# Hybrid decoder step on one core: the last pair of column blocks as block products, the reciprocal root's chain on VectorE, the layer vectors loaded early and turned later

## The chip, the cores and the metric

The kernel runs on one core of a Trainium2 chip, as one program. The metric is the device time of an execution in microseconds (us). A core has TensorE (PE in the profile; PEld is its weight load), VectorE (DVE), ScalarE (ACT), GpSimd (POOL) and SyncE (SP), each with an instruction queue of its own that it works through in order; they meet at semaphores.

## What is computed

Two layers of a decoder, for a prompt of 512 tokens and 8 samples of 4 tokens (544 tokens in all), model width 1024, feed-forward width 2816. In float32:

```python
def layer_norm(x, g, b):
    mu = mean(x); var = mean(square(x - mu))
    return (x - mu) * rsqrt(var + LN_EPS) * g + b

def swiglu(x, w_up, w_down):
    a, u = split(x @ w_up, 2)
    return (silu(a) * u) @ w_down

def decoder_layer(x, ...):
    x = layer_norm(ALPHA * x + 0.5 * swiglu(x, ffn1_up, ffn1_down), ln1_g, ln1_b)
    q, k, v, glu, gates = split(x @ w_in + b_in)
    attn = window_attention(q, k, v, sinks)            # 128 tokens back, ALiBi
    c = silu(layer_norm(causal_depthwise(u_a * sigmoid(u_g)), conv_ln_g, conv_ln_b))
    mix = sigmoid(g_attn) * (attn @ w_attn_out) + sigmoid(g_conv) * (c @ w_conv_out)
    x = layer_norm(ALPHA * x + mix @ w_out, ln2_g, ln2_b)
    x = layer_norm(ALPHA * x + 0.5 * swiglu(x, ffn2_up, ffn2_down), ln3_g, ln3_b)
```

The outputs are the activations and the new caches (keys, values, convolution state) of both groups.

## The kernel before

The activations stand transposed: features on the 128 partitions, the 544 tokens in the free dimension, as four tiles of two feature blocks each. Token halves are 272 wide (`CUT`; in the last FFN's end 288 and 256). Every large product is done three times over split numbers: weights and activations are each split into a high part (a cast to fp32r by ScalarE) and a low part (what is left, by a subtraction on VectorE), and high x high, high x low and low x high are summed in PSUM.

A *plain unit* (`unit`, L451 to L453) is one piece of 256 weight columns times one token half: for each of `kk` blocks of 128 input features and each of two column blocks of 128, three matmuls. A piece is fetched by SP and split by `prep` (L291, L292). `W` takes prepared pieces in order and prepares `la` pieces ahead; `ahead(n)` does so at a fixed place.

*FFNs.* Of the four FFNs three are *fast* (`is_fast`: all but layer 0's first). All start with `up_first`: the column blocks 0 and 1 of `a` and `u` as plain units. Then, in a fast FFN, `middle` walks through `fast_order`. An entry `s(j, m)` is a *product run*: 128 columns of `a` and the same 128 of `u`. The weights are read as 2 x 2 block matrices (the two input blocks of a pair, by `a` and `u`), the activations likewise (the two input blocks, by the two token halves), and their product takes seven block products instead of eight. The activations' four combinations for it are the tiles `T`, made in the stage before by `right`; the weights' combinations are made by `steps`. `up_fast` issues a run: one matmul that opens a buffer (L678), then the seven products (L664; each 4 x 3 matmuls of 272 columns), with copies, sums and the SiLU between them (L682 to L696). The returned `rest` (L702, L460, L461) multiplies the gate and splits the result into `H`. An entry `dn` is a plain unit of the down projection, over one group of column pairs (`GROUPF`, the last group holds three pairs, `kk` = 6). Pairs 2 to 9 are done by product runs. Pair 10 follows as plain units: `a` 10 and `u` 10, both halves each (192 matmuls). Then `tail` does the last group's `dn` units, first half before second, with the layer norm.

*The planner.* In `middle` the preparation is cut into steps with a cost on ScalarE and VectorE (`steps`) and a number of buffers. `fill(us)`, called behind each product and unit, advances a time and emits steps as long as their summed costs keep up with it and `room` is left; `room` counts free buffers of the pool `pair` (37 buffers). `V` takes the next prepared piece and forces steps if it isn't ready. `more` keeps three pieces fetched, up to the piece `stop`. Instructions of `middle` are kept in program order; elsewhere (also in `tail`) a scheduler orders each engine's instructions by an estimate of its own, when the program is built. That order is fixed when it runs.

*Layer norm.* `ln_fin` gives three steps, emitted a set distance apart while the next units are issued (`put_off`, `due`; the distances are `D_LN`, in units in which one block of six matmuls counts 0.7) or at the stage's end (`flush`): `centre` sums over the partitions with a matmul (L482), subtracts the mean (L487) and squares; `newton` sums the squares (L500, matmuls L504) and calls `rsqrt`; `scale` spreads the root over the partitions with matmuls (L512), multiplies (L516) and hands on to `ln_out` (gain and bias L549, splits L460, L461). `rsqrt` works on at most 128 x 3 numbers: three instructions on VectorE (L526 to L528: add epsilon, and the seed from the number's bits), then eleven on POOL (L530 to L540), each of which but the first needs the one before. There are 16 roots: 14 from `ln_fin`, two in `final`, the output stage, which turns the last sums back (L878), takes statistics (L880, L886) and applies mean, gain, root and bias (L893, L902).

*Layer vectors.* `setup_layer` loads the layer's gains, biases, convolution weights and sinks by small DMAs on POOL's queue (L983 to L1015), turns them with TensorE (L992, L1001) into PSUM buffers of the pool `ps1` (two buffers) and copies them out with VectorE (L994, L1002); a third use of `ps1` holds a small matmul (L1012). Its source tiles come from the pool `f1` (ten buffers). `mark` calls it behind `up_first` in the first FFN of a layer; in layer 1 it also issues the cache shifts.

## Time and profile before

| | us |
|---|---|
| median of 3 runs | 2626.16 |
| lowest, highest | 2626.13, 2630.38 |
| the profiled execution | 2630.69 |
| its span, first to last instruction | 2628.7 |

The profile is of one execution. Its rows are times from the span's start. A row of the timeline gives start, duration, engine, line, operation, what it writes and reads, how many instructions are merged, and in brackets the idle time before it with what ended it. TensorE's matmuls overlap, so the distance between two starts, not the duration, is what one costs. [...]

### The profile page before, as it was taken

To read this page: it belongs to the slowest core of one execution; us is meant where nothing else is said; L and a number is where in the kernel's file an instruction comes from. 1 tells how busy PE (TensorE), PEld (TensorE's weight loads), DVE (VectorE), ACT (ScalarE), POOL (GpSimd) and SP (SyncE) were. 2 spreads that over 40 slices of the span, in tenths; PEclk is the share of its full clock that TensorE was granted. 3 is DMA by queue.
4 is the path that set the end of the run, shared out by engine and by line. 5 is a ranking of instruction groups with operands and counts; after the bars stand their busy time and mean duration, and the time that the engine had idled before them with its cause. 6 is when DMAs were issued, how large, how long until landed. Compare 5 with 4: busy or idle time off the path is not lost.

```text
span 2628.7 us, 47397 instructions
## 1 busy us (share of the span) xinstructions
PE 2552.5 (97%) x20110; PEld 2502.8 (95%) x20110; DVE 1715.0 (65%) x2567; ACT 1126.2 (43%) x1972; POOL 298.0 (11%) x499
## 2 busy tenths in 40 slices
PE   8999999999999999999989999989999999999996
PEld 7999999988999999999989999989899999999996
DVE  4333237797986567666556666549979766676645
ACT  4222124477526254443344443245773353444431
POOL 2000001722301000000020000017232000000001
PEclk8999999999999999999989999989999999999998
DMA  7223133231322213332422333312214222233331
GB/s 219 83 89 104 54 109 85 50 95 53 101 65 87 91 58 96 97 97 89 133 75 82 97 97 97 116 49 76 82 53 113 69 81 87 78 93 97 97 101 39
DMA packets 302628, 232.15 MB, mean 88 GB/s; under 512 B 43812, under 2 KB 300020, under 8 KB 302320
## 3 DMA queue, kind: packets, MB, share of 16 engines
q1 hardware_dynamic: 298576, 220.37, 27.8%
q0 software_dynamic: 3840, 8.76, 1.1%
q8 instruction: 157, 2.57, 0.4%
q14 instruction: 55, 0.45, 0.1%
HBM read 225.69 MB, written 9.16 MB: 89 GB/s over the span
## 4 chain that ended last, share of the span: by engine, by line
PE 82%; DVE 8%; POOL 4%; ACT 3%; issue 2%; DMA 1%; DVEq 0%; POOLq 0%; ACTq 0%
PE pa L453 20%; PE pa L451 20%; PE pa L452 20%; PE pa L664 11%; PE pb L664 8%; DVE pr L1126 3%; POOL f L1141 2%; DVE wl L292 1%; DVE pr L461 1%; PE pb L1266 1%; DVE at L1247 1%; PE pa L1237 1%; PE pb L1278 1%; ACT at L1251 1%; PE pb L512 0%
## 5 line engine op out<-in xcount | busy, mean ns | idle before, releaser
L451 PE MATMUL pa<-pr,wh 128*128 128x272 f32 (+1 forms) x4032 | 1176.1, 293 | 18.7 <-ACT pr L460 11.1
L453 PE MATMUL pa<-pr,wl 128*128 128x272 f32 (+1 forms) x4032 | 1173.4, 292 | 4.9 <-DVE wl L292 4.9
L452 PE MATMUL pa<-pr,wh 128*128 128x272 f32 (+1 forms) x4032 | 1170.3, 291 | 3.7 <-DVE pr L461 3.6
L451 PEld LDWEIGHTS pa<-pr,wh 128*128 128x128 f32 x4032 | 765.8, 190 | 26.0 <-ACT pr L460 13.5
L452 PEld LDWEIGHTS pa<-pr,wh 128*128 128x128 f32 x4032 | 771.5, 191 | 8.2 <-DVE pr L461 6.0
L453 PEld LDWEIGHTS pa<-pr,wl 128*128 128x128 f32 x4032 | 765.6, 190 | 6.1 <-DVE wl L292 5.7
L292 DVE TENSOR_TENSOR wl<-raw,wh 128x1024 fp32r<-128x1024 f32 (+1 forms) x268 | 309.8, 1183 | 77.3 <-ACT wh L291 54.0
L1126 DVE SCALAR_TENSOR_TENSOR pr<-u,cw,pr 128x512 f32<-128x512 f32 x480 | 344.4, 764 | 2.2 <-ACT pr L1119 2.0
L291 ACT CAST wh<-raw 128x1024 fp32r<-128x1024 f32 (+1 forms) x268 | 259.9, 1009 | 159.8 <-PE pa L453 90.9
L453 PE MATMUL pa<-pr,wd 128*128 128x272 f32 x768 | 221.8, 289 | 0.0
L451 PE MATMUL pa<-pr,wd 128*128 128x272 f32 x768 | 221.4, 288 | 0.0
L452 PE MATMUL pa<-pr,wd 128*128 128x272 f32 x768 | 220.8, 288 | 0.0
L717 DVE SCALAR_TENSOR_TENSOR pr<-pa,pr 128x544 f32<-128x544 f32 (+2 forms) x152 | 109.7, 722 | 153.5 <-PE pa L453 152.7
L530 POOL TENSOR_SCALAR nw<-nw 91x3 f32<-91x3 f32 (+2 forms) x16 | 5.6, 349 | 1703.2 <-DVE nw L526 1703.2
L460 ACT CAST pr<-f 128x544 fp32r<-128x544 f32 (+1 forms) x124 | 79.7, 647 | 216.4 <-DVE f L611 116.1
L664 PE MATMUL pa<-pr,wa 128*128 128x272 f32 x1152 | 160.9, 289 | 0.0
L664 PE MATMUL pb<-pr,ws 128*128 128x272 f32 x1152 | 159.6, 288 | 0.0
L664 PEld LDWEIGHTS pa<-pr,wa 128*128 128x128 f32 x1152 | 151.4, 188 | 0.0
L664 PEld LDWEIGHTS pb<-pr,ws 128*128 128x128 f32 x1152 | 150.0, 188 | 0.0
L452 PEld LDWEIGHTS pa<-pr,wd 128*128 128x128 f32 x768 | 145.1, 189 | 0.0
L451 PEld LDWEIGHTS pa<-pr,wd 128*128 128x128 f32 x768 | 144.5, 188 | 0.0
L453 PEld LDWEIGHTS pa<-pr,wd 128*128 128x128 f32 x768 | 144.3, 188 | 0.0
(225 smaller groups left out, 3139.6 us busy)
## 6 DMA issues: line engine op xcount, KB each, us to landing
raw<-in_ffn_up_dram SPq DMA_DIRECT2D x174, 512.0 KB, 4.4
raw<-in_ffn_down_dram SPq DMA_DIRECT2D x76, 512.0 KB, 3.6
raw<-in_w_in_dram SPq DMA_DIRECT2D x72, 512.0 KB, 4.1
raw<-in_w_in_dram SPq DMA_DIRECT2D x64, 128.0 KB, 3.0
raw<-in_w_attn_out_dram SPq DMA_DIRECT2D x32, 256.0 KB, 4.0
raw<-in_w_conv_out_dram SPq DMA_DIRECT2D x16, 512.0 KB, 3.4
raw<-in_w_out_dram SPq DMA_DIRECT2D x16, 512.0 KB, 4.3
raw<-in_ffn_down_dram SPq DMA_DIRECT2D x24, 256.0 KB, 2.8
```

The costliest lines, as they stand in the source:

```text
L291: ins = self.nc.scalar.copy(wh, t)
L292: self.nc.vector.tensor_tensor(wl, t, wh.bitcast(F32), op=ALU.subtract)
L451: pin(self.nc.tensor.matmul(o, lhsT=wh, rhs=h, start=k == 0, stop=False))
L452: pin(self.nc.tensor.matmul(o, lhsT=wh, rhs=lo, start=False, stop=False))
L453: pin(self.nc.tensor.matmul(o, lhsT=wl, rhs=h, start=False, stop=k == kk - 1))
L460: pin(self.nc.scalar.copy(hi, src))
L461: pin(self.nc.vector.tensor_tensor(lo, src, hi.bitcast(F32), op=ALU.subtract))
L664: mm = lambda a, b, first=False, last=False: pin(nc.tensor.matmul(o, lhsT=a, rhs=b, start=first, stop=last, skip_group_check=True))
L717: pin(nc.vector.scalar_tensor_tensor(Y[p][:, :, hs], ps, 0.5, Y[p][:, :, hs], op0=ALU.mult, op1=ALU.add))
L1126: self.last["cw"] = nc.vector.scalar_tensor_tensor(cc[:, m, 0:SEQ], u[:, m, k:k + SEQ], cw[:, 8 * k + c:8 * k + c + 1], cc[:, m, 0:SEQ], o ...
L1141: nc.gpsimd.tensor_tensor(pr[:, 4 * b:4 * b + 4, :], win, wv.unsqueeze(1).to_broadcast([128, DS, KC]), op=ALU.mult)
L1237: nc.tensor.matmul(s[:, 2 * r + t, :], lhsT=q, rhs=k, start=t == 0 and ps == 0, stop=ps == 2, skip_group_check=True)
```

## The change

- `fast_order` ends with the two product runs `s(10, 0)` and `s(10, 1)` in place of `a` 10 and `u` 10; `middle` walks through them too, the plain units of pair 10 and the method `P` are gone, and the planner's `stop` takes in the last group's four `dn` pieces, which `pre` now takes with `V` instead of preparing them with `ahead(4)`.
- `rsqrt` issues its eleven instructions on VectorE instead of POOL.
- `setup_layer` issues its DMAs and returns a function `turn` that does the transposes, copies and the small matmul. In a fast FFN (layer 1) the loads are issued ahead of `up_first` and `turn` and the cache shifts come behind it; in layer 0 both come where they came before. The two halves of the convolution weights share one tile, and the sinks' small tile has a tag of its own.

```diff
--- before.py
+++ after.py
@@ fast_order
-        return o + [("a", 10), ("u", 10)] + [("dn", 4, p, 0) for p in range(4)]
+        return o + [s(10, 0), s(10, 1)] + [("dn", 4, p, 0) for p in range(4)]
...
@@ rsqrt
         self.nc.vector.tensor_scalar(i32(r), i32(t), -1.0, float(RS_SEED), op0=ALU.mult, op1=ALU.add)
-        g = self.nc.gpsimd
+        g = self.nc.vector
         g.tensor_scalar_mul(u, v, RS_B * RS_B)
...
@@ ffn, begin
-            self.stop = self.pi + len(self.ffn_order(l, f)) - 10
+            self.stop = self.pi + len(self.ffn_order(l, f)) - 4
...
@@ ffn, middle
-            for kind, *k in self.fast_order()[4:-6]:
+            for kind, *k in self.fast_order()[4:-4]:
...
@@ ffn
         if self.is_fast(l, f):
             gl = len(GROUPF) - 1
+            turn = self.mark(l, f)
             up_first()
             Y += self.scaled(Y0)
-            self.mark(l, f)
+            turn()
             middle()
             if last:
                 self.cut = FB[FK[1][0]][0]
-            wa = self.P(l, f, "a", 10)
-            h = new_h(gl)
-            sa = [silu(wa, 0)]
-            self.ahead(2)
-            sa.append(silu(wa, 1))
-            wu = self.W(l, f, "u", 10, la=1)
-            gated(wu, h, 0, sa[0])
-            self.ahead(2)
-            gated(wu, h, 1, sa[1])
             ws = []
 
             def pre(hf):
                 if hf == 0:
-                    self.ahead(4)
-                    ws.extend(self.W(l, f, "dn", gl, p, la=1) for p in range(4))
+                    ws.extend(self.V(l, f, "dn", gl, p) for p in range(4))
                 else:
                     self.ahead(A3)
...
@@ ffn, the other branch
-                    self.mark(l, f)
+                    self.mark(l, f)()
...
@@ mark
-        if f == "ffn1":
-            if l == 0:
-                self.setup2()
-            self.setup_layer(l)
+
+        if f != "ffn1":
+            return lambda: None
+        if l == 0:
+            self.setup2()
+        turn = self.setup_layer(l)
+
+        def rest():
+            turn()
             if l:
                 self.shift_caches(l)
+        return rest
...
@@ setup_layer
-        ps = self.p1()
-        nc.tensor.transpose(ps[:, :NVEC], rows[:NVEC, :], self.ident[:NVEC, :NVEC])
-        vec = t([128, NVEC], F32, f"vec{l}")
-        nc.vector.tensor_copy(vec, ps[:, :NVEC])
-        cw = t([128, KC * 8], F32, "cw")
         wr = a["conv_dw_w"][l].rearrange("k (c p) -> (k c) p", p=128)
-        ps = self.p1()
+        wrows = self.f1(shape=[128, 2, 128])
         for h in range(2):
-            rows = self.f1(shape=[128, 128])
-            nc.gpsimd.dma_start(rows[:124, :], wr[124 * h:124 * h + 124, :])
-            nc.tensor.transpose(ps[:, 124 * h:124 * h + 124], rows[:124, :], self.ident[:124, :124])
-        self.after(nc.vector.tensor_copy(cw, ps[:, :248]), "cw")
+            nc.gpsimd.dma_start(wrows[:124, h, :], wr[124 * h:124 * h + 124, :])
...
-        sk4 = self.sp.tile([128, 4], F32, tag="nw", name=self.nm("nw"))
+        sk4 = self.sp.tile([128, 4], F32, tag="sk", name=self.nm("sk"))
...
+
+        def turn():
+            ps = self.p1()
+            nc.tensor.transpose(ps[:, :NVEC], rows[:NVEC, :], self.ident[:NVEC, :NVEC])
+            vec = t([128, NVEC], F32, f"vec{l}")
+            nc.vector.tensor_copy(vec, ps[:, :NVEC])
+            cw = t([128, KC * 8], F32, "cw")
+            ps = self.p1()
+            for h in range(2):
+                nc.tensor.transpose(ps[:, 124 * h:124 * h + 124], wrows[:124, h, :], self.ident[:124, :124])
+            self.after(nc.vector.tensor_copy(cw, ps[:, :248]), "cw")
+            nc.vector.tensor_scalar_mul(nsk, nsk, -1.0)
+            nsks = t([128, 4], F32, f"nsks{l}")
+            ps = self.p1()
+            nc.tensor.matmul(ps[:, :4], lhsT=sel, rhs=sk4[:4], start=True, stop=True)
+            nc.vector.tensor_copy(nsks, ps[:, :4])
...
+        return turn
```

## Rows read from the trace of the kernel before

**Rows 1.** The page, busy time of each engine with its share of the span and its instructions.

```profile
PE 2552.5 (97%) x20110; PEld 2502.8 (95%) x20110; DVE 1715.0 (65%) x2567; ACT 1126.2 (43%) x1972; POOL 298.0 (11%) x499
```

**Rows 2.** Timeline of TensorE over one product run: its first matmul (L678) and the first behind the run.

```profile
2509.93 0.29 PE L678 MATMUL pb<-pr,wa 128*128 128x272 f32 x1
...
2520.59 0.29 PE L451 MATMUL pa<-pr,wd 128*128 128x272 f32 x1
```

**Rows 3.** Groups of instructions by line, whole span: busy us, mean ns of one, then the idle time before them with what ended it.

```profile
L664 PE MATMUL pa<-pr,wa 128*128 128x272 f32 x1152 | 160.9, 289 | 0.0
...
L312 DVE TENSOR_TENSOR wa<-raw,wa 128x1024 fp32r<-128x1024 f32 x48 | 58.6, 1221 | 53.5 <-ACT wa L322 35.9 <-PE pa L664 17.7
...
L312 DVE TENSOR_TENSOR f<-raw,raw 128x512 f32<-128x512 f32 x48 | 32.8, 683 | 0.0
```

**Rows 4.** Who TensorE waited for, whole span: us in total, times, longest.

```profile
PE pb L512 <- POOL nw L540: 17.3, 7, 4.5
```

**Rows 5.** Stretches behind waits: from and to, length, busy us (and instructions) of PE, PEld, DVE, ACT, POOL, then the granted clock, DMA share and GB/s.

```profile
448.60:452.00 3.40, 3.40 (x29) 3.40 (x30) 2.49 (x4) 1.73 (x4) 0.00 (x0) 1.00 1.01 261
827.30:830.70 3.40, 3.40 (x17) 3.40 (x17) 2.20 (x4) 3.37 (x5) 0.00 (x0) 0.50 0.00 0
957.00:963.80 6.80, 6.29 (x26) 5.97 (x27) 5.91 (x10) 6.06 (x10) 0.00 (x0) 0.50 0.01 2
2121.00:2124.30 3.30, 3.30 (x17) 3.30 (x16) 3.30 (x5) 3.29 (x5) 0.00 (x0) 0.50 0.00 0
2250.70:2254.00 3.30, 3.03 (x14) 2.70 (x13) 2.58 (x6) 3.30 (x7) 0.00 (x0) 0.50 0.02 5
```

**Rows 6.** Timeline of TensorE at its waits: the matmul that waited, with the idle time before it.

```profile
421.40 0.79 PE L512 MATMUL pb<-ident,nw 91*128 91x91 f32 x5 [0.94 <-POOL nw L540]
...
448.57 0.68 PE L512 MATMUL pb<-ident,nw 91*128 91x91 f32 x4 [1.83 <-POOL nw L540]
...
827.07 1.18 PE L512 MATMUL pb<-ident,nw 91*128 91x91 f32 x5 [2.04 <-POOL nw L540]
...
957.45 0.82 PE L451 MATMUL pa<-pr,wh 128*128 128x272 f32 x2 [2.84 <-ACT pr L460]
...
1319.08 1.16 PE L512 MATMUL pb<-ident,nw 91*128 91x91 f32 x4 [4.33 <-POOL nw L540]
...
1381.64 0.38 PE L1012 MATMUL pb<-nw,f 4*128 4x4 f32 x2 [2.97 <-DVE vec L994]
...
1739.48 0.57 PE L512 MATMUL pb<-ident,nw 91*128 91x91 f32 x3 [1.60 <-POOL nw L540]
...
2120.02 0.34 PE L512 MATMUL pb<-ident,nw 91*128 91x91 f32 x1 [2.05 <-POOL nw L540]
...
2250.36 0.39 PE L451 MATMUL pa<-pr,wh 128*128 128x272 f32 x1 [2.85 <-ACT pr L460]
```

**Rows 7.** Stretches at the end of the first fast FFN: the old pair 10, and the first-half `dn` units behind it (columns as in rows 5).

```profile
1251.50:1275.60 24.10, 24.10 (x195) 24.10 (x194) 8.30 (x10) 4.82 (x7) 0.00 (x0) 1.00 0.35 111
1275.60:1293.70 18.10, 18.10 (x146) 18.10 (x145) 9.77 (x12) 4.54 (x6) 0.00 (x0) 1.00 0.54 174
```

**Rows 8.** Timeline of POOL, late links of the root of 819 us.

```profile
823.85 1.12 POOL L536 TENSOR_TENSOR nw<-nw,nw 91x3 f32<-91x3 f32 x1
...
826.54 0.20 POOL L539 TENSOR_SCALAR nw<-nw 91x3 f32<-91x3 f32 x1
```

**Rows 9.** Timeline of VectorE in the same window.

```profile
819.15 0.16 DVE L526 TENSOR_SCALAR nw<-pb 91x3 f32<-91x3 f32 x1 [1.10 <-PE pb L504]
819.41 0.17 DVE L527 TENSOR_SCALAR nw<-nw 91x3 int32<-91x3 int32 x1
...
819.78 2.63 DVE L461 TENSOR_TENSOR pr<-pr,pr 128x544 fp32r<-128x544 f32 x4
822.43 3.69 DVE L586 SCALAR_TENSOR_TENSOR pr<-pr,pr 128x1088 f32<-128x1088 f32 x3
```

**Rows 10.** Timeline of the root of 947 us: its first instruction on VectorE, its last on POOL, and L512 on TensorE.

```profile
947.38 0.16 DVE L526 TENSOR_SCALAR nw<-pb 91x3 f32<-91x3 f32 x1 [3.83 <-PE pb L504]
...
950.65 0.19 POOL L540 TENSOR_TENSOR nw<-nw,nw 91x3 f32<-91x3 f32 x1
...
953.15 0.47 PE L512 MATMUL pb<-ident,nw 91*128 91x91 f32 x3
```

**Rows 11.** Timeline of VectorE at the roots of 797 and 1315 us.

```profile
796.64 0.15 DVE L526 TENSOR_SCALAR nw<-pb 91x3 f32<-91x3 f32 x1
796.82 0.17 DVE L527 TENSOR_SCALAR nw<-nw 91x3 int32<-91x3 int32 x1
...
1315.37 0.15 DVE L526 TENSOR_SCALAR nw<-pb 91x3 f32<-91x3 f32 x1
1315.48 0.44 DVE L480 TENSOR_TENSOR pr<-pr 128x272 f32<-128x272 f32 x1
...
1316.11 0.17 DVE L528 TENSOR_SCALAR nw<-nw 91x3 int32<-91x3 int32 x1
```

**Rows 12.** Timeline of VectorE in the output stage.

```profile
2606.10 4.05 DVE L902 SCALAR_TENSOR_TENSOR at<-at,nw,at 128x512 f32<-128x512 f32 x6 [1.56 <-POOL nw L540]
```

**Rows 13.** Timeline at layer 1's vectors: the last load's issue on POOL, and the first copy on VectorE.

```profile
1358.07 0.51 POOL L1011 DMA_DIRECT2D f<-in_c_sel_dram  x1
...
1381.32 0.27 DVE L994 COPY vec<-pb 128x116 f32<-128x116 f32 x1
```

More of the change, by code (lines that the diff above doesn't have):

```diff
@@ L430, in W @@
         return ms, kk
-    def P(self, *key):
-        self.ahead(2)
-        return self.W(*key, la=1)
     def unit(self, w, xs, hf, pin=lambda i: i):
@@ L758, in ffn @@
                 self.cut = FB[FK[1][0]][0]
-            wa = self.P(l, f, "a", 10)
-            h = new_h(gl)
-            sa = [silu(wa, 0)]
-            self.ahead(2)
-            sa.append(silu(wa, 1))
-            wu = self.W(l, f, "u", 10, la=1)
-            gated(wu, h, 0, sa[0])
-            self.ahead(2)
-            gated(wu, h, 1, sa[1])
             ws = []
@@ L1002, in setup_layer @@
-        self.after(nc.vector.tensor_copy(cw, ps[:, :248]), "cw")
+            nc.gpsimd.dma_start(wrows[:124, h, :], wr[124 * h:124 * h + 124, :])
         nsk = t([128, NH], F32, f"nsk{l}")
         nc.gpsimd.dma_start(nsk, a["attn_sinks"][l:l + 1, :].to_broadcast([128, NH]))
-        nc.vector.tensor_scalar_mul(nsk, nsk, -1.0)
-        nsks = t([128, 4], F32, f"nsks{l}")
-        sk4 = self.sp.tile([128, 4], F32, tag="nw", name=self.nm("nw"))
+        sk4 = self.sp.tile([128, 4], F32, tag="sk", name=self.nm("sk"))
@@ L1008, in setup_layer @@
         nc.gpsimd.dma_start(sk4[:4], a["attn_sinks"][l].rearrange("(n t) -> t n", t=4))
-        ps = self.p1()
         sel = self.f1([4, 128])
         nc.gpsimd.dma_start(sel, a["c_sel"])
-        nc.tensor.matmul(ps[:, :4], lhsT=sel, rhs=sk4[:4], start=True, stop=True)
-        nc.vector.tensor_copy(nsks, ps[:, :4])
         bv = t([128, DKV], F32, "bv")
         self.after(nc.gpsimd.dma_start(bv, a["b_in"][l:l + 1, O_V:O_V + DKV].to_broadcast([128, DKV])), "bv")
-        self.vec.append(vec)
@@ L1017, in setup_layer @@
-        self.cw.append(cw)
-        self.nsk.append(nsk)
-        self.nsks.append(nsks)
-        self.bv.append(bv)
+        def turn():
[13 more added lines that the diff above has]
+            nc.vector.tensor_copy(nsks, ps[:, :4])
+            self.vec.append(vec)
+            self.cw.append(cw)
+            self.nsk.append(nsk)
+            self.nsks.append(nsks)
+            self.bv.append(bv)
```

## The prediction

> **What bounds the kernel now.** I read the page first, then the waits of TensorE, then the places of those waits in order of time. The page says that TensorE has instructions in flight for 97% of the span [rows 1], so only two things can shorten this kernel: fewer matmuls, or fewer moments in which TensorE stands still. The matmuls of the block products run back to back: one product run, with its copy matmul, is 85 matmuls in 2520.59 - 2509.93 = 10.66 us, 0.1254 us each [rows 2], and no product matmul waited for a weight (idle 0.0 in the group's row [rows 3]). The waits that are left are few. The largest kind is the matmul that spreads the reciprocal root (L512) waiting for POOL's chain, 17.3 us at 7 places [rows 4]. [...]
>
> Two kinds of place must be kept apart. At five places (421.40, 448.57, 827.07, 1739.48, 2120.02) TensorE has other work and goes on with it right after L512, so it waited only because L512 stood too early in its fixed order: 0.94 + 1.83 + 2.04 + 1.60 + 2.05 = 8.5 us [rows 6]. The other two (4.33 us at 1319.08 and the one of 4.5 us, 1714.87) are the ends of fast FFNs, where nothing else is left [rows 4, 6].
>
> **Part 1, the last pair as block products.** It takes away, in each of three fast FFNs, `a` 10 and `u` 10 as plain units: 2 pieces x 2 halves x 8 steps x 2 column blocks x 3 = 192 matmuls. It adds two product runs of 85, so 170. The difference is 22 x 0.1254 = 2.76 us, three times 8.3 us, all on the path, since TensorE does not pause in the 24.1 us of the old pair [rows 7]. What could eat it is the preparation. A run's weights cost VectorE 3 subtractions of 1.22 and 5 of 0.68 us [rows 3], 7.1 us, where the two plain pieces cost four subtractions together; with the evacuation and the first two of the four `dn` pieces some 10 us of VectorE work then stand in each run of 10.66 us at most. The planner's counters (costs and room) let me follow where each step is written: every step of the second run's weights is written within the first run, the last one some 7 us before its first use, and two `dn` pieces during the second run; the other two are needed 9 us (two units of 36 matmuls) later. VectorE has the room: it is busy 8.3 of 24.1 us in the old pair and 9.8 of 18.1 in the stretch behind it [rows 7]. So I take 8.3 us. Bounds: 8.3, and nothing if the preparation is late by a whole saving. The units behind the pair need its `H` only from their 31st matmul on, 3.8 us; the cover is the same as before.
>
> **Part 2, the root's chain on VectorE.** Eleven small POOL instructions per root, 16 roots. Left alone, POOL starts one every 0.28 us, but while VectorE runs instructions with two inputs each takes as long as the one on VectorE: 1.12 us at 823.85 beside L586, 0.20 at 826.54 when VectorE is free [rows 8, 9]. That is what makes the five waits: the chain of 819.15 ends when L512 starts, at 827.07, 7.9 us later; the free one of 947.38 ends at 950.84, 3.5 us later; and TensorE comes to L512 some 6 us after L526 in both (827.07 - 2.04 = 825.03, and 953.15) [rows 6, 9, 10]. The order on the engines is thus written with a chain of nearly 6 us in mind, and what VectorE does to POOL is not in it.
>
> What does a link cost on VectorE? Its own three links start 0.18 us apart (796.64, 796.82) or 0.26 (819.15, 819.41) [rows 9, 11]; I take both as ends, so fourteen links are 2.5 to 3.6 us. [...]
>
> A free chain is thus no shorter on VectorE than on POOL. Where VectorE has other work ready, the scheduler puts it between two links (L480 at 1315.48, behind L526 at 1315.37; the small one then adds 0.11 us) [rows 11]. In the window of 819.15 seven such instructions (6.3 us) would stand between links [rows 9]; with 0.8 us for the seven links and four more at 0.18 to 0.26 the chain ends at 827.6 to 827.9, later than POOL's. The gain at the five places is not a faster chain; it is that VectorE's queue is one the order counts, so that L512 is written behind other matmuls. Bounds for the five: 8.5 us gained, or 5 x 0.8 = 4 us lost if the order stays. The links' spread is 1.1 us; I leave a wait of 0.5 us at each place, so 6.0 us gained. The two places with 2.04 and 2.05 us were followed by 3.4 us of half clock each, the one of 1.83 us by none [rows 5, 6]. So 3.4 us more come back.
>
> A gain that the diff does not name: in the covered cases POOL is done 2.3 us before TensorE comes to L512 (950.84 against 953.15 [rows 10]). At the end of `mix` that lateness is paid: the first matmul of the next FFN on the second half waits 2.84 us (957.45) and 2.85 (2250.36) for the splits that follow [rows 6], with 6.8 and 3.3 us of half clock [rows 5]. With 14 links L512 could stand at 949.9 to 951.0, 2.0 us or more earlier, which leaves under 0.9 us: 2 x 2.0 + 5.1 = 9.1 us. Whether the order moves so far no row shows; bounds 0 and 9.1, I take half, 4.5.
>
> At the two ends of fast FFNs VectorE is free after 1316.28 [rows 11]; eleven links end at 1318.3 to 1319.1 against L512's start at 1319.08 [rows 6]: I take nothing, 0.8 us each at most. At the kernel's end VectorE itself is late: L902 starts at 2606.10 after 1.56 us of idle time and holds up the last sum [rows 12]. That idle time has room for six to eight links of eleven, and each link set between other work costs 0.11 us there; so L902 starts up to 1 us later, and the second root once more. I take 0.7 us lost (0 to 1.8). Beside these the chain adds 16 x 11 links to VectorE, 20 to 45 us of 1715 busy; the engine is at 65% [rows 1] and who queues behind a link waits 0.1 us.
>
> **Part 3, the layer vectors.** At layer 1 the transposes wait no more for loads, whose last issue is at 1358.07 [rows 13]; TensorE's wait there is another one: L1012, third user of two PSUM buffers, waits 2.97 us for VectorE's copy L994, queued behind the planner's subtractions until 1381.32 [rows 6, 13]. Earlier loads let the transposes stand right behind `up_first`; the two buffers and the queue stay. The DMA issues of 0.5 us each move on POOL's queue ahead of `up_first`; POOL has no chain to hold up any more. The three tiles are held longer out of ten `f1` buffers, where the second half's layer norm takes its squares and the FFN its gates. Bounds 3.0 gained, 1 lost; I take half the wait, 1.5 us gained. At layer 0 nothing moves but the DMA order.
>
> **Sum.** 8.3 + 6.0 + 3.4 + 4.5 + 1.5 - 0.7 = 23.0 us. The profiled execution took 2630.7 us (span 2628.7), so 2607.7 by its own time. The runs' median is 2626.2, 4.5 us less; against it the forecast is 2603.2.
>
> **The rivals.** (a) Only the products pay: the order puts L512 as much too early for the new chain as for the old, and the waits stay. For it: the links are no faster. Against it: the five waits stand only where POOL was slowed. Gain 8.3 - 0.7 = 7.6, so 2618.6. Chance 0.17.
> (b) The last pair is starved: two runs follow each other without the two `dn` units (12 us) that mostly lie between runs, and TensorE waits for L312 or for a buffer. Against it: 0.0 us in the runs so far [rows 3], two of which, `s(2, 1)` and `s(3, 0)`, also follow each other, and the counters above. If it eats the whole saving, 23.0 - 8.3 = 14.7, so 2611.5. Chance 0.10.
> (c) Slower: the order prices the small links too low. L512 is emitted 18 matmuls (3 steps of 6, 2.3 us) behind L504; if the scheduler believes in a chain that short, TensorE stands there while VectorE needs 3.6 us in seven places that are now covered (1.3 us each, 9.1) and about 8.3 in the five busy ones (6 us each in place of 1.7, 21.5), and five waits of that size cost half clock of 3.4 us or more (8.5). 9.1 + 21.5 + 8.5 - 8.3 = 31 us, 2657. It decides from a mean wait of about 1.4 us at these twelve places (12 x 1.4 = 8.5 + 8.3). Against it: in the seven covered places the order left 2.3 us too much, not too little. Chance 0.07.
> The forecast has 0.63, and 0.03 is for what I don't see.
>
> **How the numbers follow.** The predicted time is the forecast's, 2603. Low end: all terms at their better bounds, 8.3 + 8.5 + 3.4 + 9.1 + 3.0 + 1.6 for the two ends, 33.9, so about 2592. High end: rival (a) and a little of lost preparation, 2621. About 0.2% (5 us) is what can be told from no change here. Faster by more: nearly all of the forecast and of (b), most of (a), 0.82. Within: 0.10. Slower: (c) and a point, 0.08.
>
> **What would show it.** Part 1: 66 matmuls fewer, no idle time at the last two runs, and 21.3 in place of 24.1 us for the pair. Part 2: no wait of L512 above 1 us outside the two ends of FFNs, full clock behind 827 and 2120, L512 less than 6 us behind L504, the waits at the ends of `mix` under 1 us; POOL's busy time down. Waits of 1.5 us or more at L512 in places that had none would be rival (c); waits on L312 in the last runs, (b). Part 3: the wait at L1012 under 1.5 us. I would be wrong in kind if new waits show up at `f1` buffers or if the ends of the FFNs, where VectorE's queue decides, come out otherwise than before.

## The result and the profile after

The changed kernel took 2615.0 us (median of 6 runs, 2612.4 to 2617.7) beside 2628.3 us for the kernel before (2626.0 to 2630.9): a ratio of 0.9950, 95% interval 0.9937 to 0.9963, so 13 us less, between 10 and 17. The forecast was 23 us less; its range holds the result. The profiled execution was 2612.4 us (span 2610.6). The two profiled spans lie 18.1 us apart, more than the medians: the mean granted clock is 0.981 in the trace of before and 0.985 in that of after, so half clock cost about 50 us in the one and 39 in the other (an estimate: the span times the share not granted).

Line numbers have moved: L512 is now L507, L504 is L499, L526 to L540 are L521 to L535, L482 is L477, L451 to L453 are L446 to L448, L460 is L455, L461 is L456, L480 is L475, L516 is L511, L586 is L581, L664 is L659, L902 is L894, L717 is L712, L1012 is L1010. Below, times in us behind "at" are places in the span.

Busy time of the engines on the page of after, beside [rows 1]:

```profile
PE 2539.1 (97%) x20044; PEld 2489.3 (95%) x20044; DVE 1769.1 (68%) x2791; ACT 1142.5 (44%) x2008; POOL 238.8 (9%) x323
```

TensorE has 66 instructions fewer, and POOL's 16 x 11 links (499 - 323 = 176) have gone to VectorE. Who TensorE waited for in after, whole span (us in total, times, longest), beside [rows 4]:

```profile
PE pa L446 <- ACT pr L455: 16.0, 6, 2.8
PE pb L507 <- DVE nw L535: 9.9, 3, 3.7
PE pb L477 <- DVE pr L475: 4.5, 3, 3.8
```

The wait for the root's chain went from 17.3 us at 7 places to 9.9 at 3. That looks like a gain of 7 us, until one asks where the other waits stand. TensorE's timeline in after, the waiting matmuls with their idle time, and L507 at two roots where it did not wait; beside [rows 6]:

```profile
427.41 0.82 PE L477 MATMUL pb<-pr,ones 128*128 128x272 f32 x1 [3.82 <-DVE pr L475]
...
452.04 0.32 PE L507 MATMUL pb<-ident,nw 91*128 91x91 f32 x1 [2.60 <-DVE nw L535]
...
820.57 0.29 PE L499 MATMUL pb<-ones,pr 128*91 128x1 f32 x2 [0.90 <-DVE pr L495]
...
832.31 0.47 PE L507 MATMUL pb<-ident,nw 91*128 91x91 f32 x3
...
836.62 0.59 PE L446 MATMUL pa<-pr,wh 128*128 128x272 f32 x1 [2.85 <-ACT pr L455]
...
955.68 0.69 PE L507 MATMUL pb<-ident,nw 91*128 91x91 f32 x5
...
959.99 0.39 PE L446 MATMUL pa<-pr,wh 128*128 128x272 f32 x1 [2.59 <-ACT pr L455]
...
1315.63 0.49 PE L507 MATMUL pb<-ident,nw 91*128 91x91 f32 x1 [3.53 <-DVE nw L535]
...
1375.59 0.27 PE L1010 MATMUL pb<-sk,f 4*128 4x4 f32 x1 [1.01 <-DVE vec L1001]
```

At four of the five contended roots the wait did not go, it moved and grew: 0.94 became 3.82 (now at the next half's mean, L477), 1.83 became 2.60, 2.04 became 0.90 + 2.85 and 2.05 became 0.89 + 2.85 (now at the sums L499, ahead of the root, and mostly at the next unit, L446). (The second pair is at 2100 and 2116, as at 820 and 836.) Only the 1.60 at 1739 is gone. Together 8.5 us became 13.9. The waits at the ends of `mix` stayed (2.84 to 2.59, with 0.46 at L447 right behind, where before has 0.27 at most), those at the ends of the two fast FFNs lost 0.8 us each (3.53 at 1315, 3.75 at 1705), and L1010 lost 2.0.

What is late there? VectorE in after at the contended root of 821, from its first link on, beside [rows 9]:

```profile
821.22 0.16 DVE L521 TENSOR_SCALAR nw<-pb 91x3 f32<-91x3 f32 x1 [0.80 <-PE pb L499]
...
821.89 0.71 DVE L456 TENSOR_TENSOR pr<-pr,pr 128x544 fp32r<-128x544 f32 x1
822.53 0.15 DVE L527 TENSOR_TENSOR nw<-nw,nw 91x3 f32<-91x3 f32 x1
822.60 0.72 DVE L456 TENSOR_TENSOR pr<-pr,pr 128x544 fp32r<-128x544 f32 x1
...
827.65 1.28 DVE L581 SCALAR_TENSOR_TENSOR pr<-pr,pr 128x1088 f32<-128x1088 f32 x1
828.85 0.15 DVE L535 TENSOR_TENSOR nw<-nw,nw 91x3 f32<-91x3 f32 x1
```

Small, large, small, large: seven foreign instructions between fourteen links, 7.8 us from first start to last end, where POOL took 7.9 [rows 6, 9]. This much the prediction had said. What it had not is the 3.3 us between the last link's end, 829.00, and L507 at 832.31. The free root shows the same gap:

```profile
950.09 0.16 DVE L521 TENSOR_SCALAR nw<-pb 91x3 f32<-91x3 f32 x1 [3.77 <-PE pb L499]
...
952.43 0.16 DVE L535 TENSOR_TENSOR nw<-nw,nw 91x3 f32<-91x3 f32 x1
```

Fourteen links in 2.5 us, and L507 3.1 us behind them, 5.6 behind the first link; before it was 5.8 [rows 10]. From L507 to the first matmul that needs the scaled half it is 4.3 us at all these places (832.31 to 836.62, 955.68 to 959.99; before, 953.15 to 957.45 [rows 6, 10]). So a late L507 is handed on whole.

The root of 441 is another case. L507 waits for its chain there (2.60 us at 452.04), for the chain takes 11.2 us (440.66 to 451.89) where POOL's took 7.7 (440.77 to 448.51). One of the foreign instructions brought a wait of its own into it:

```profile
446.09 1.23 DVE L292 TENSOR_TENSOR wl<-raw,wh 128x1024 fp32r<-128x1024 f32 x1 [1.31 <-ACT wh L291]
```

VectorE stood still for ScalarE, with a link next in its queue. The chains of 412 and 1722 grew too, from 7.3 to 9.9 and from 6.4 to 8.4 us.

Stretches behind the waits of after (columns as in rows 5):

```profile
426.45:433.27 6.82, 5.86 (x24) 5.63 (x25) 6.18 (x11) 6.82 (x14) 0.00 (x0) 0.50 0.00 0
453.76:457.17 3.41, 3.41 (x19) 3.41 (x18) 2.53 (x4) 3.41 (x7) 0.00 (x0) 0.50 0.82 283
836.10:839.50 3.40, 2.88 (x13) 2.89 (x14) 1.99 (x4) 3.40 (x7) 0.00 (x0) 0.50 0.07 26
959.99:966.80 6.81, 6.35 (x48) 6.13 (x49) 5.92 (x10) 5.61 (x9) 0.00 (x0) 1.00 0.01 2
```

The granted clock is 0.50 behind these three of the contended waits, and behind the one at 2116 as well. There a matmul of 272 columns starts every 0.227 us (2117.14 to 2119.18, nine of them) where at full clock one takes 0.125 [rows 2], so 45% of such a stretch is lost; the forecast's terms and the estimates here take half. Behind the 2.59 us at 959.99 it is 1.00, and behind the 2.84 us at 957 before it was 0.50 [rows 5]: one place, nearly one wait, two clocks.

### The profile page after: what moved, and what is told of

The parts are those of the page before. It is cut to its first block, busy times and chain, and to the rows that moved or that the text cites. A ratio compares the mean times of both kernels' runs of the same rounds, so it can differ in the third digit from the quotient of the medians.

```text
span 2610.6 us, 47286 instructions
## 1 busy us (share of the span) xinstructions
PE 2539.1 (97%) x20044; PEld 2489.3 (95%) x20044; DVE 1769.1 (68%) x2791; ACT 1142.5 (44%) x2008; POOL 238.8 (9%) x323
## 4 chain that ended last, share of the span: by engine, by line
PE 84%; DVE 8%; ACT 4%; POOL 2%; issue 1%; DMA 1%; SPq 0%; DVEq 0%; POOLq 0%; ACTq 0%
PE pa L446 19%; PE pa L448 19%; PE pa L447 19%; PE pa L659 12%; PE pb L659 9%; DVE pr L1123 3%; POOL f L1138 2%; DVE wl L292 1%; DVE pr L456 1%; PE pb L1263 1%; DVE at L1244 1%; PE pa L1234 1%; DVE pr L511 1%; PE pb L1275 1%; ACT at L1248 1%
## 5 line engine op out<-in xcount | busy, mean ns | idle before, releaser
L446 PE MATMUL pa<-pr,wh 128*128 128x272 f32 x3552 | 1036.0, 293 | 22.5 <-ACT pr L455 16.0
L448 PE MATMUL pa<-pr,wl 128*128 128x272 f32 x3552 | 1033.1, 291 | 4.1 <-DVE wl L292 4.1
L447 PE MATMUL pa<-pr,wh 128*128 128x272 f32 x3552 | 1029.1, 290 | 4.3 <-DVE pr L456 4.3
L446 PEld LDWEIGHTS pa<-pr,wh 128*128 128x128 f32 x3552 | 673.5, 190 | 30.0 <-ACT pr L455 18.4
L447 PEld LDWEIGHTS pa<-pr,wh 128*128 128x128 f32 x3552 | 678.5, 191 | 8.4 <-DVE pr L456 6.4
L448 PEld LDWEIGHTS pa<-pr,wl 128*128 128x128 f32 x3552 | 673.2, 190 | 5.1 <-DVE wl L292 4.8
L292 DVE TENSOR_TENSOR wl<-raw,wh 128x1024 fp32r<-128x1024 f32 x232 | 274.9, 1207 | 65.5 <-ACT wh L291 41.9
L448 PE MATMUL pa<-pr,wd 128*128 128x272 f32 (+2 forms) x1056 | 305.2, 289 | 0.0
L446 PE MATMUL pa<-pr,wd 128*128 128x272 f32 (+2 forms) x1056 | 303.6, 288 | 0.0
L447 PE MATMUL pa<-pr,wd 128*128 128x272 f32 (+2 forms) x1056 | 303.4, 288 | 0.0
L291 ACT CAST wh<-raw 128x1024 fp32r<-128x1024 f32 x232 | 229.9, 1025 | 147.3 <-PE pa L448 91.2
L712 DVE SCALAR_TENSOR_TENSOR pr<-pa,pr 128x544 f32<-128x544 f32 (+2 forms) x152 | 109.6, 723 | 144.7 <-PE pa L448 143.6
L447 PEld LDWEIGHTS pa<-pr,wd 128*128 128x128 f32 x1056 | 199.5, 189 | 0.0
L448 PEld LDWEIGHTS pa<-pr,wd 128*128 128x128 f32 x1056 | 198.3, 188 | 0.1
L446 PEld LDWEIGHTS pa<-pr,wd 128*128 128x128 f32 x1056 | 198.3, 188 | 0.1
L659 PE MATMUL pa<-pr,wa 128*128 128x272 f32 x1296 | 181.0, 289 | 0.0
L659 PE MATMUL pb<-pr,ws 128*128 128x272 f32 x1296 | 179.6, 288 | 0.0
L659 PEld LDWEIGHTS pa<-pr,wa 128*128 128x128 f32 x1296 | 170.3, 188 | 0.0
L659 PEld LDWEIGHTS pb<-pr,ws 128*128 128x128 f32 x1296 | 168.7, 188 | 0.0
L455 ACT CAST pr<-f 128x544 fp32r<-128x544 f32 x124 | 79.6, 647 | 187.3 <-DVE f L606 87.5
L456 DVE TENSOR_TENSOR pr<-f,pr 128x544 fp32r<-128x544 f32 x124 | 89.1, 723 | 79.4 <-ACT pr L455 79.3
```

The source lines that it names most:

```text
L291: ins = self.nc.scalar.copy(wh, t)
L292: self.nc.vector.tensor_tensor(wl, t, wh.bitcast(F32), op=ALU.subtract)
L446: pin(self.nc.tensor.matmul(o, lhsT=wh, rhs=h, start=k == 0, stop=False))
L447: pin(self.nc.tensor.matmul(o, lhsT=wh, rhs=lo, start=False, stop=False))
L448: pin(self.nc.tensor.matmul(o, lhsT=wl, rhs=h, start=False, stop=k == kk - 1))
L455: pin(self.nc.scalar.copy(hi, src))
```

## The experiments

All ratios are to the kernel before, timed beside it, with their 95% interval; us are the ratio times 2629 (the change itself: 13 us less). A difference between two of these kernels is good to some 4 to 7 us, and the granted clock goes with the time: among the 23 runs of the kernel before that stand beside part 1 alone, part 2 alone, parts 1 and 3, and the ten links, spans are 2621 to 2624 us at a mean clock of 0.985 and 2632 at 0.980, so some 1.7 us per 0.001 (an estimate).

**One part alone, or one left out.** Part 1 alone: `fast_order`, `begin` and the last pair as after, the rest as before. Against after, in part:

```diff
-        g = self.nc.vector
+        g = self.nc.gpsimd
...
-            turn = self.mark(l, f)
             up_first()
             Y += self.scaled(Y0)
-            turn()
+            self.mark(l, f)
```

> The kernel before with part 1 alone (last pair of column blocks as block products; the root stays on POOL, the layer vectors as before). Theory: the products pay 66 matmuls of 0.1254 us, 8.3 us in place, and nothing is late, so 8.3 us less than before, and the waits of L512 in the five contended places stay as they were (8.5 us). Rival (the prepared weights come late): part of the 8.3 us is eaten by waits at the last two product runs, and the kernel gains 0 to 5 us.

Measured: 0.9976 (0.9965 to 0.9988), 6.3 us less. TensorE in that kernel, from the end of `mix` to the end of the next fast FFN:

```profile
954.89 0.59 PE L446 MATMUL pa<-pr,wh 128*128 128x272 f32 x1 [2.85 <-ACT pr L455]
...
1313.53 0.52 PE L507 MATMUL pb<-ident,nw 91*128 91x91 f32 x1 [4.24 <-POOL nw L535]
```

358.64 us where before has 1319.08 - 957.45 = 361.63 [rows 6]; 0.09 of the 2.99 is the shorter wait at the end, so 2.9 for the products, where 2.76 had been forecast. The product groups of after (L659) have no idle time. Three times 2.9 is 8.7, inside the interval; that the median says only 6.3 goes with the mean clock of its runs, 0.980 beside 0.983, some 4 us by the estimate above. No starving.

Part 2 alone, against before:

```diff
-        g = self.nc.gpsimd
+        g = self.nc.vector
         g.tensor_scalar_mul(u, v, RS_B * RS_B)
```

> The kernel before with part 2 alone: the root's eleven links on VectorE. The forecast's terms for it add up to 6.0 + 3.4 + 4.5 - 0.7 = 13.2 us gained. Theory from the trace of after: at the five contended places one other VectorE instruction stands between nearly every two links, the chain is as long as POOL's, and the waits there grow by about 5 us with 5 us more of half clock; against it the ends of mix lose their half clock (5 us), the ends of the fast FFNs gain 0.8 us each and the kernel's end 4 us. Together about 1 us gained, between 4 gained and 3 lost.

Measured: 1.0005 (0.9997 to 1.0014), 1.3 us more. The forecast's 13.2 us are refuted; the rough balance of losses and gains holds. One gain stands at no wait of TensorE: from the first link of the kernel's last two roots to the end of the span it is 23.9 us here and 27.5 before. Parts 1 and 3 without part 2 (the same line the other way round, in after):

> The kernel after with the root's eleven links back on POOL, so parts 1 and 3 without part 2. Theory: 8.3 us for the products and 2.0 for the layer vectors (the wait of the transposes at layer 1 goes from 2.97 to about 1.0 us), so 10.3 us less than before and 1 to 3 us more than after: the root's move is worth next to nothing on its own. Rival (the forecast): the root's move carries 13.2 us, and without it the kernel is some 13 us slower than after.

Measured: 0.9951 (0.9940 to 0.9962), 12.9 us less. Moving the root added nothing that can be measured to this. The two agree: part 2 is worth nothing that can be measured (between 0.8 us gained and 3.7 lost), as a sum of terms that are not zero, and the change is its parts 1 and 3.

Part 3 alone, and after without part 3. The part's edit in `ffn`, against before (the rest of it is in `mark` and `setup_layer`):

```diff
+            turn = self.mark(l, f)
             up_first()
             Y += self.scaled(Y0)
-            self.mark(l, f)
+            turn()
```

> The kernel before with part 3 alone (layer vectors loaded ahead of the first units and turned behind them). Theory from the traces: the wait of the matmul L1010 falls from 2.97 to 1.0 us, so 2 us less than before, and what the run with parts 1 and 3 gained beyond part 1 alone (6.6 us by the medians, with 4 us of uncertainty) is mostly half clock that differs from one run to the next. Rival: the loads off the way are worth 5 us or more in themselves (the stages of the two layers' starts, where the traces of the two runs differ by 3.3 us each).

> The kernel after without part 3, so block products and the root on VectorE, with the layer vectors as before. Theory from the traces: part 3 is worth the 2.0 us by which the wait of the transposes shrinks, and 1.7 us for the half clock that followed that wait in two of three traces, so this run is 2 to 4 us slower than after (9 to 11 less than before). Rival (as the run with part 3 alone says, 6.8 less than before): 6 to 8 us slower than after, that is 5 to 7 less than before.

Measured: 0.9974 (0.9963 to 0.9986), 6.8 us less; and 0.9968 (0.9957 to 0.9979), 8.4 us less, so 4.7 less than the change with it. With the step from part 1 to parts 1 and 3 (12.9 - 6.3 = 6.6) there are three readings of part 3, each good to some 4 us: 6.8, 6.6, 4.7. My 2 us was too small. Behind the wait of the transposes the clock differs; after without part 3, from the end of the wait on, and then part 3 alone:

```profile
1379.30:1382.70 3.40, 3.40 (x17) 3.40 (x16) 0.00 (x0) 1.79 (x2) 0.00 (x0) 0.50 0.02 5
```

```profile
1371.50:1377.00 5.50, 5.44 (x43) 5.43 (x44) 3.62 (x9) 3.66 (x5) 0.00 (x0) 1.00 0.11 31
```

With the wait of 2.97 us three of four traces have 3.4 us of half clock there, with 1.01 us none: 2.0 + 1.7 = 3.7 us are accounted for. The mean granted clock is 0.979 to 0.982 in the four traces without part 3 and 0.983 to 0.988 in the nine with it, but the other half-clock stretches lie elsewhere from trace to trace, and over all runs the clocks overlap (0.978 to 0.985 without, 0.979 to 0.988 with it). At like clock, by the estimate above, the three readings become some 6, 3 and 2 us, around the 3.7 accounted for.

**Fewer links.** The same root in 10 links:

```diff
-        g.tensor_scalar_mul(u, v, RS_B * RS_B)
+        k = -0.375 * RS_B
         g.tensor_tensor(t, r, r, op=ALU.mult)
-        g.tensor_tensor(t, t, v, op=ALU.mult)
-        g.tensor_scalar(t, t, -1.0, RS_A, op0=ALU.mult, op1=ALU.add)
-        g.tensor_tensor(r, r, t, op=ALU.mult)
+        g.scalar_tensor_tensor(t, t, k, v, op0=ALU.mult, op1=ALU.mult)
+        g.scalar_tensor_tensor(r, t, k * RS_A, r, op0=ALU.subtract, op1=ALU.mult)
...
+        g.scalar_tensor_tensor(r, v, 1.875 / 0.375, r, op0=ALU.add, op1=ALU.mult)
```

> The kernel after with the same root computed in 10 links in place of 14 on VectorE (products with a constant folded into scalar_tensor_tensor instructions; same computation up to rounding). Theory, one other instruction enters between two links where VectorE has work ready: 4 links fewer take 4 x 0.7 to 1.2 us out of each contended chain, some 3.5 us, and the order sets L507 earlier (in TensorE's order 55 to 66 matmuls behind the sums where after has 69 to 89, in four of the five places; 39 to 42 in place of 45 to 48 where VectorE is free). The waits of these places, 13.9 us, should fall to about 6, the free chains gain 0.7 us each at the three ends of fast FFNs and the two ends of mix: 8 to 15 us less than after. Rival (what is late behind the contended roots is all that is queued on VectorE, not the chain): the waits stay, and the gain is 0 to 4 us, from the ends alone.

Measured: 0.9907 (0.9895 to 0.9919), 24.4 us less, 11 less than after. VectorE at the contended root (815 here):

```profile
815.74 0.16 DVE L527 SCALAR_TENSOR_TENSOR nw<-nw,nw 91x3 f32<-91x3 f32 x1
815.91 0.73 DVE L456 TENSOR_TENSOR pr<-pr,pr 128x544 fp32r<-128x544 f32 x1
816.55 0.15 DVE L528 SCALAR_TENSOR_TENSOR nw<-nw,nw 91x3 f32<-91x3 f32 x1
...
818.86 0.16 DVE L532 SCALAR_TENSOR_TENSOR nw<-nw,nw 91x3 f32<-91x3 f32 x1
```

Four foreign instructions in place of seven, and 4.1 us (814.95 to 819.01) in place of 7.8: with four links fewer, three foreign instructions fewer entered. But the waits did not fall to 6 us. They are 3.51 + 1.29 + 2.62 + 2.62 = 10.0, those at the ends of `mix` even rose to 2.97, and at the roots of 815 and 945 L507 still stands 2.7 and 2.9 us behind the chain's end (819.01 to 821.74, 946.48 to 949.38). So the lateness behind the chain is a matter of its own. Of the 11 us, 3.9 are these waits, 1.3 the ends of the FFNs (2.87 and 3.15); the mean clock, 0.986 for 0.985, is some 2.6 us; the rest is within the uncertainty.

**Where L507 stands.** How many matmuls stand between L499 and L507 in TensorE's order, counted in the traces (a matmul is 0.125 us):

```
root at (after)      412  441  798  821  919  950  1722
before                51   44   50   47   47   47    39
after                 87   69   48   89   45   45    85
ten links             87   66   42   55   39   39    61
after, L507 placed    87   69   48   66   45   25    85
ten links, placed     73   56   42   36   39   19    61
the same, later       87   66   42   46   39   19    61
```

The order did count VectorE's queue: 89 for 47 at 821. It just leaves some 3 us more than the chip needs, in the free case too: 45 matmuls are 5.6 us for a chain of 2.5. Four links fewer moved L507 by 6 matmuls, 0.75 us, 0.19 per link, which is what a link takes; the 3 us thus look like a constant beside the links. Why the order leaves them is not shown, and it does not everywhere: in after L507 stands 0.9 us behind the chain's end at 412, 2.2 at 1722, and too early at 441. So I set L507 by hand, with an edge that keeps later unit matmuls behind it, and touched nothing else (`PLACE` gives the number of the root and how many unit matmuls written behind L507 may still go ahead of it):

```diff
+PLACE = {3: 146, 5: 99, 11: 146, 13: 99}
...
+    def hold(self, ins):
+        if self.held:
...
+            if self.held[1] < 0:
+                self.tc.add_manual_dep(
+                    ins.ins, self.held[0].ins.name,
+                    mybir.DependencyInfo(mybir.DependencyClass.NoSync, mybir.DependencyReason.DATA), reason="place")
```

> The kernel after, with only the place of L507 in TensorE's order changed for four roots (the second halves of the convolution's norm and of the norm at the end of mix, both layers): 66 and 25 matmuls behind the sums L499 where after has 89 and 45, by an edge that puts the later unit matmuls behind it. The same instructions stand between the links as in after. Theory: in after L507 starts 3.0 to 3.2 us later than the chain's last link ends, because the order takes the chain for longer than it is, and the waits of L446 some 4 to 7 us behind it (2.85, 2.59, 2.85, 2.60 us) are that lateness handed on; set 2.5 to 2.9 us earlier they fall to under 0.6 each: 9 us, and up to 5 us of half clock, less than after. Rival (the splits behind L507 are late because of what is queued on ScalarE and VectorE): the waits stay where they are, or come back at L507 itself, and nothing changes (2 us either way).

Measured: 0.9904 (0.9891 to 0.9918), 25.2 us less, 12 less than after. TensorE in that kernel (L522 is L507, L448 and L449 are L446 and L447):

```profile
831.61 0.58 PE L522 MATMUL pb<-ident,nw 91*128 91x91 f32 x4
...
836.94 0.40 PE L448 MATMUL pa<-pr,wh 128*128 128x272 f32 x1 [0.97 <-ACT pr L468]
...
952.20 0.47 PE L522 MATMUL pb<-ident,nw 91*128 91x91 f32 x3
...
957.25 0.39 PE L448 MATMUL pa<-pr,wh 128*128 128x272 f32 x1 [0.21 <-DVE f L623]
958.24 0.40 PE L449 MATMUL pa<-pr,wh 128*128 128x272 f32 x1 [0.59 <-DVE pr L469]
```

The chains are as long as in after (7.78 and 2.50 us, ends at 831.21 and 951.66), L507 follows after 0.4 to 0.5 us, and the waits are 0.97 for 2.85 and 0.21 + 0.59 for 2.59 + 0.46, at layer 1 the same. That is 8.3 us, and the late L507 is shown as the cause of these four waits. The half clock behind two of them is gone too, which is worth 3.4 us, but other stretches came in this trace: its mean clock is 0.984 for 0.985 and its span only 6.4 us shorter than that of after. So 8.3 of the 12 us are shown, and the rest goes with a clock that differs from run to run. Both remedies together:

> The 10-link chain with L507 placed by hand for five roots at the end of the chain as the run with the short chain showed it (73, 36, 19, 36, 19 matmuls behind L499 in place of 87, 55, 39, 55, 39). Theory: its waits of 3.51, 2.62, 2.97, 2.62 and 2.98 us fall by 1.7, 2.5, 2.4, 2.5, 2.4: some 11 us less than with the short chain alone, so about 36 us less than before. Rival, as for the run that places L507 for the long chain: no change against the short chain alone (24.5 us less than before).

Measured: 0.9897 (0.9882 to 0.9912), 27.1 us less where 36 had been expected; beside the ten links alone it is 2.7 less, too little to be told from nothing. At the convolution's root the wait grew to 5.48 us. ScalarE there (the norm's activations are L1488, a gate's L1414):

```profile
828.79 1.12 ACT L1488 ACTIVATE pr<-pr,vec 128x272 f32<-128x272 f32 x2
829.93 1.28 ACT L1414 ACT_TABLE_LOAD   x1
831.23 0.86 ACT L1414 ACTIVATE pr<-pa,vec 128x272 f32<-128x272 f32 x2
832.10 1.28 ACT L1488 ACT_TABLE_LOAD   x1
...
837.37 2.28 ACT L468 CAST pr<-pr 128x544 fp32r<-128x544 f32 x4
```

L507 came so early that the scheduler put a gate's activations among the norm's, with two more table loads. From the norm's first activation to the first split (L468) it is 8.6 us, 828.79 to 837.37, where the ten links alone have 4.1 (825.48 to 829.54): two loads of 1.28, the gate's 0.86 and a cast of weights, 1.03, make up the 4.5 that were added. In these rows the next activation starts 0.02 us behind a load's end (829.93 + 1.28 to 831.23), so here a switch is 1.3. The second placing leaves the gate in front (against the run before):

```diff
-PLACE = {0: 94, 3: 115, 5: 102, 11: 115, 13: 102}
+PLACE = {3: 125, 5: 102, 11: 125, 13: 102}
```

> The 10-link chain with L507 placed by hand at four roots: 46 matmuls behind L499 at the convolution's second halves (the first try had 36, the order itself takes 55) and 19 at the ends of mix (the order takes 39). Theory: at 36 L507 came ahead of a gate's activation, and ScalarE went through two more table loads on the way to the splits (the wait grew from 2.62 to 5.48 us); at 46 the table loads are as with the short chain alone (34 in all in place of 38), the waits fall to about 1.5 us each there and to 0.6 at the ends of mix. 2 x 1.1 + 2 x 2.4 = 7 us less than with the short chain alone, some 31 us less than before. Rival (the early L507 costs as much elsewhere on VectorE or ScalarE): no change against the short chain alone, 24 to 25 us less than before.

Measured: 0.9875 (0.9857 to 0.9894), 32.9 us less where 31 had been expected. The number came out near, but not by its terms. The waits at the ends of `mix` fell from 2.97 to 0.48 + 0.59 each, 3.8 of the 8.5 us by which it lies below the ten links; the convolution's wait stayed at 2.61, though L507 stands 9 matmuls earlier. The rest goes with the granted clock, 0.985 to 0.988 in these runs and 0.983 to 0.986 with the ten links; whether the shorter waits brought that is not shown (the profiled execution, at 0.985, spans 2600.6 us, that of the ten links 2601.1). ScalarE there:

```profile
828.62 0.86 ACT L1414 ACTIVATE pr<-pa,vec 128x272 f32<-128x272 f32 x2
829.49 1.28 ACT L1488 ACT_TABLE_LOAD   x1
830.78 2.13 ACT L1488 ACTIVATE pr<-pr,vec 128x272 f32<-128x272 f32 x4
832.82 1.04 ACT L293 CAST wh<-raw 128x1024 fp32r<-128x1024 f32 x1
833.76 2.13 ACT L1488 ACTIVATE pr<-pr,vec 128x272 f32<-128x272 f32 x4
835.79 2.28 ACT L468 CAST pr<-pr 128x544 fp32r<-128x544 f32 x4
```

From the gate to the first split ScalarE does not pause, 828.62 to 835.79, 7.17 us; with the ten links alone it is the same 7.17 (822.37 to 829.54), with the cast at another point. Here ScalarE's queue is what is late, not L507.

**Which engine at which root.** Against after:

```diff
+        self.nr = getattr(self, "nr", -1) + 1
-        g = self.nc.vector
+        g = self.nc.vector if self.nr in (6, 8, 14, 15) else self.nc.gpsimd
```

> The kernel after with the root's 14 links on VectorE only in four of the sixteen roots, where VectorE has little else: the first halves behind the two fast FFNs that end with a wait (L507's 4.3 and 4.5 us), and the two of the kernel's end; on POOL in the twelve others. Theory: the contended places cost VectorE's chain some 10 us more than POOL's and the uncontended ends give 4 to 6 us back; so 4 to 6 us less than with all roots on POOL (12.9 less than before), about 18 us less than before and some 4 less than after. The forecast's own terms for these places (nothing at the ends of FFNs, 0.7 us lost at the kernel's end) would make it 1 us slower than with all roots on POOL.

Measured: 0.9927 (0.9914 to 0.9939), 19.2 us less, 6 less than with POOL everywhere. The two traces show 5 of it: 1.3 at the ends of the fast FFNs (3.54 and 3.89 for 4.24 and 4.45) and 3.6 from the first link of the last two roots to the end of the span (23.7 for 27.3). What VectorE gains at these four roots and what it gives up where it is busy can thus be had apart. Last, ten links with L507 placed, and the first two roots on POOL:

```diff
+        if self.nr < 2:
+            g, u = self.nc.gpsimd, new()
...
+            return r
```

> As the run before it in this call, with the first two roots (first FFN of layer 0, where VectorE is busiest) on POOL's 11 links again. Theory: these two stages took 26.5 us between the roots with POOL's chain and 28.5 with either chain on VectorE; 2 us less than with all roots on VectorE, some 33 us less than before. Rival: the waits of L507 on POOL there (0.9 and 1.8 us) and the half clock behind them eat it, no change.

Measured: 0.9858 (0.9841 to 0.9875), 2592.6 us, 37.3 us less: the fastest of all. It is 4.4 less than with the second placing, where 2 had been expected, but the two intervals overlap. Its waits for the root, by the same view as above:

```profile
PE pb L522 <- DVE nw L564: 6.1, 2, 3.2
...
PE pb L522 <- POOL nw L555: 2.7, 2, 1.8
```

The 6.1 us are the ends of the two fast FFNs, where nothing else is left for TensorE.

## Why the prediction was right, and where not

The time lay in the range, but not by the forecast's own sum: one part came out as forecast, one at nothing and one larger, so part of it is luck.

- **Part 1**, 8.3 us: right. 2.9 us per fast FFN in the trace in place of 2.76, no wait at the product runs; alone 6.3 (3.2 to 9.2).
- **The five contended places**, 6.0 us gained: wrong, 5.4 lost, and this is the step that failed. The prediction had a chain no shorter than POOL's (8.5 to 8.8 us forecast, 7.8 measured) and the order's counting of the queue right. It then took for granted that a counted queue puts L507 at the chain's end, and that a matmul moved back costs nothing. The order put it 3 us behind the end, 42 matmuls later than before at 821, and its consumer stayed where it was, 1.5 us of work behind it. Placing L507 earlier took those waits from 2.85 to 0.97. At 452.04 the chain itself was 3.5 us longer than POOL's; the prediction had let the root of 819.15 stand for all five. At 427.41 it is another queue: L477 waited for L475, which stood on VectorE behind the four scalings L511:

```profile
424.39 2.61 DVE L511 TENSOR_TENSOR pr<-pr,pb 128x544 f32<-128x544 f32 x4
426.92 0.44 DVE L475 TENSOR_TENSOR pr<-pr 128x272 f32<-128x272 f32 x1
```

- **Half clock behind 827 and 2120**, 3.4 us gained: wrong, since these waits did not go. 3.4 us of it stand behind 836 and 2116 again, and 6.8 and 3.4 more behind 426 and 453.
- **The ends of `mix`**, 4.5 us (half of 9.1): the waits fell by 0.25 us each, not by 2.0. The order stayed, which the prediction had named as the lower bound. That the half clock behind them was missing in this trace is no step of mine: a wait of nearly the same length has 6.8 us of it in before (2.84 at 957) and none in after (2.59 at 959.99).
- **The ends of fast FFNs**, nothing, 0.8 us each at most: the bound came true, 0.8 twice.
- **The kernel's end**, 0.7 us lost: wrong in sign, 3.8 gained. From the first link of the first of these roots to the end of the span it is 2610.6 - 2586.87 = 23.7 us, before 2628.7 - 2601.20 = 27.5. Only 0.4 of it lies ahead of the last group of L894 (2604.00 - 2586.87 = 17.13, before 2618.76 - 2601.20 = 17.56). VectorE put the last sum ahead of the first L894 (in before it stood behind):

```profile
2593.00 0.69 DVE L712 SCALAR_TENSOR_TENSOR pr<-pa,pr 128x512 f32<-128x512 f32 x1 [1.05 <-PE pa L448]
2593.60 4.04 DVE L894 SCALAR_TENSOR_TENSOR at<-at,nw,at 128x512 f32<-128x512 f32 x6
```

The last turns wait 0.35 us for 3.09, but L894 is as much later. The other 3.3 us stand behind the landing of the output's last store. Behind its last instruction POOL closes the program with a DRAIN; here are its drains in before and in after (number, shortest, median and longest in ns, first and last start):

```profile
L1551 POOLq DRAIN  x3: 98/194/8991, 2618.5 to 2628.3; - x3
...
L1548 POOLq DRAIN  x3: 46/97/9321, 2555.1 to 2610.3; - x3
```

The first is the long one in both. In before it starts with POOL's last link and lasts until 2627.5, 3 us past the landing of the last store at 2624.5, and the kernel ends behind it. In after POOL has no links, and the drain is over at 2564.4, long before the last landing at 2609.7. All four traces with POOL's chain at the end (before, part 1 alone, part 3 alone, parts 1 and 3) end 4.0 to 4.2 us behind the last landing, the nine others 0.9 to 1.0. The prediction had looked at VectorE's queue alone.

- **Part 3**, 1.5 us: too small. The wait fell by 2.0, the half clock behind it is worth 1.7, and the three comparisons say 4.7 to 6.8, or 2 to 6 at like clock.

So part 2, 13.2 us of the forecast, is worth nothing: 5.4 us lost at the contended places and about 1 in small waits that grew (L447 behind the ends of `mix`, L477 near 932 and 2212) stand against 3.8 gained at the kernel's end, 1.6 at the ends of the FFNs and 0.5 at the ends of `mix`. By this sum 0.5 us are lost, and part 2 alone measured 1.3 lost. Part 3 is worth more than forecast. Rivals (a), 2618.6, and (b), 2611.5, had nearer sums, each for a wrong reason: no product run was starved, and L507 stands mostly not too early but too late. With that rival (c), the order pricing the links too low, is refuted as well; only at the root of 441 does L507 stand too early.

## What to carry to other kernels

A wait that leaves its old line has not gone until the next one downstream is read: add up the waits of a place, not of a line. An in-order engine that takes other work between the links of a dependent chain pays for them, here mostly one foreign instruction per link and the waits of these instructions too (7.8 us for fourteen links that alone take 2.5), so shorten the chain before moving it. And compare where a scheduler puts the consumer of a chain with the chain's real end: an edge that sets it there was worth as much here as the whole change (12 us beside 13). Last, read what stands behind the last store: an engine that works late can hold up the program's end, here by 3 us.

## What the hardware showed that I had not expected

A link of 91x3 on VectorE is followed by the next dependent one after 0.19 us (14 links in 2.50 us), inside the prediction's 0.18 to 0.26. But set between large instructions it adds only 0.07 us, where the prediction had 0.11: four L456 in a row take 2.63 us, so they start 0.64 apart [rows 9], and 0.71 apart with a link between (821.89, 822.60). A chain on a busy VectorE is thus dear in waiting and nearly free in engine time. POOL's drain took 9.0 us behind its last link in before, and the four kernels with POOL's chain at the end finish 3 us later behind their last landing than the nine others. And the same 2.6 to 2.9 us of wait at one place was followed by 6.8 us of half clock in one trace and none in another, so a term for half clock behind a single wait is uncertain by its whole size.
